# Eight plain first feed-forward tiles before twelve Strassen-Winograd pairs, the last gate's modulation inside the second product, and one more slot for weights

## Chip, cores and metric

The kernel runs on one core of a Trainium2 chip. The time is device microseconds of one execution. Three runs of the kernel before took 1071.28, 1064.88 and 1070.12 us; their median is 1070.12 us.

## What is computed

Two transformer blocks stand behind each other, for 512 tokens of width 1024, all in fp32. The first has 16 meta tokens ahead of the sequence, a pooling branch and an attention with forget gates; the second takes six modulation vectors (two shifts, two scales, two gates) from a conditioning vector `c`, has two kinds of attention, and a feed-forward part with a squared ReLU:

```python
def hybrid_layer(x, norm_g, w_in, b_forget, pool_w, pool_scale, w_up_pool, w_up_attn, w_out):
    h = rmsnorm(x, norm_g)
    proj = jnp.einsum('bld,dn->bln', h, w_in)
    ...
    merged = (jax.nn.sigmoid(g_pool) * jnp.einsum('blc,cd->bld', y_pool, w_up_pool)
              + jax.nn.sigmoid(g_attn) * jnp.einsum('blc,cd->bld', y_attn, w_up_attn))
    return x + jnp.einsum('bld,de->ble', merged, w_out)

def second_block(x, c, g_norm1, w_in, g_q, g_k, rel_bias, w_o, g_norm2, w1, w2, w_ada, b_ada):
    ...
        mod = c_act @ w_ada[l] + b_ada[l]
        sh1, sc1, gt1, sh2, sc2, gt2 = [m[:, None, :] for m in jnp.split(mod, 6, axis=-1)]
    ...
        x = x + gt1 * (mixed @ w_o[l])
        h = rmsnorm_2(x, g_norm2[l]) * (1.0 + sc2) + sh2
        x = x + gt2 * (jnp.square(jax.nn.relu(h @ w1[l])) @ w2[l])
```

`w_ada` is 1024 x 6144, `w1` 1024 x 4096, `w2` 4096 x 1024. The diff is about the sixth modulation vector, `gt2` (number 5 in the kernel), which is needed only at the very end, and about the products with `w1` and `w2`.

## The kernel before

**Products.** Every fp32 operand is split into a high and a low part (`split`, L130 to L132: ScalarE casts, L131, and VectorE or GpSimd subtracts, L128), and a product is three matmuls, high by high, high by low, low by high (`mm3`, L149 to L152). The order of TensorE's instructions is the order in which the code is written or woven (`manual_schedule`, `weave`); on the other engines a scheduler puts each instruction in its place, and every engine then works through its own list in order.

**Weights.** A weight tile of 512 KB comes by a DMA that SP issues into one of four slots with the tag `wr` (`weights`, L134; `w1_raw`, L1241). The cast writes one of three slots `wh`, the subtraction one of three slots `wl`. SP's list is in order too: an issue that waits for a slot holds all issues behind it.

**Modulation.** `ada(v, j)` (L203 to L217) brings one eighth of modulation vector `v`: a 512 KB load into a `wr` slot (issued at L207) and two VectorE ops, which add two rows of the weight tile, each multiplied by an entry of `c`, to the accumulator `ada` (L215 for the first, L217 for the others). After four steps one half of the vector lies there as 128 partial sums for each of 512 columns. `ada_end` (L219) sums over the partitions by TensorE (L234, eight matmul instructions in the trace for a half) and adds the bias (L237); for a gate a transpose on TensorE follows (L227), a copy, and a write to DRAM (L230), from which `load_gt` (L763) brings it back, spread over all partitions. The list `todo` holds the steps, and `ada_step(n)` takes up to n of them at set places: in block 1 vectors 0, 1, 3 and 5, three steps behind each of the eight output tiles `ups(m)` at its end; in block 2 vectors 4 and 2. `ada_all()` does what is left.

**First feed-forward product.** Its 32 tiles of 128 columns are made in two ways. A plain tile is 48 matmuls of 256 columns (`first_half`, twice). EARLY = 5 of them are done in two halves each, so that the first halves can start before the second half of the tokens is ready; one more plain tile follows. The other 26 tiles come as 13 pairs in Strassen and Winograd's form: seven products of 12 matmuls (`prod`, L1204 to L1206), 84 in all where two plain tiles have 96. For them VectorE makes four sums of the two weight tiles (`sums`, L1263 to L1266), each of which is split. A pair is `firsts` (two products), `middles` (three) and `lasts` (two), and `lasts` of a pair stands between `firsts` and `middles` of the next. `plus` (L1274 copy by ScalarE, L1275 sum by VectorE) joins two banks of PSUM into the hidden tile, and the next products that use these banks wait for it.

**Second product.** For each of 32 hidden tiles `w2_operands` loads and splits a row block of `w2` and the hidden tile, and 24 matmuls of 512 columns follow. The last two hidden tiles are done output by output, with the gate and the residual behind each.

## Time and profile before

| | us |
|---|---|
| three runs | 1064.88 to 1071.28, median 1070.12 |
| the profiled execution's own time | 1068.56 |
| its span in the trace | 1066.9 |
| TensorE busy in it | 1018.2 |
| VectorE, ScalarE, GpSimd busy | 610.4, 565.2, 297.3 |

The mean granted clock of TensorE in it is 0.992 of full speed; full speed (1.00) is 2.4 GHz, and the other level is half of it. A row of a timeline gives the start, the duration, the engine (PE is TensorE, DVE VectorE, ACT ScalarE, POOL GpSimd, SPq the list of SP), the source line, the operation with its output and inputs, and in brackets how long the engine was idle before it and what it waited for. Matmuls overlap, so the time that one costs is the distance between starts.

### The profile page before, as it was taken

The numbers are of one execution on the slowest core, as the hardware profiler recorded it, in microseconds if no ns is written. First come the engines' busy times: TensorE is split into PE (matmuls) and PEld (weight loads), VectorE is DVE, ScalarE is ACT, GpSimd is POOL, SyncE is SP. The second block draws the span as 40 slices with busy tenths as digits, with TensorE's granted clock in tenths as the row PEclk, the third lists the DMA queues.
The fourth block names the chain that finished last, engine by engine and source line by source line (L and its number), as shares of the span: only waits on it lengthen the run. The fifth ranks groups of instructions, "written<-read, shape, count | busy, mean of one in ns | idle before, by whom it ended". The sixth has DMA issues, their size and how long they took to land.

```text
span 1066.9 us, 15553 instructions
## 1 busy us (share of the span) xinstructions
PE 1018.2 (95%) x5923; PEld 862.1 (81%) x5923; DVE 610.4 (57%) x1183; ACT 565.2 (53%) x1089; POOL 297.3 (28%) x156
## 2 busy tenths in 40 slices
PE   7999999999998999899899988899899999999998
PEld 5987987778876788887678866689799998888886
DVE  5375866864365548566777577666667652111115
ACT  6365654554535646465677678446576773222221
POOL 4221124422322353112212114232222322333320
PEclk9999999999999999999999999999899999999999
DMA  8242532453564656416512134541233334233312
GB/s 239 84 119 63 150 115 80 138 162 96 157 178 131 212 181 203 141 40 179 156 53 77 50 98 134 161 119 47 81 100 111 111 88 139 79 99 99 99 60 79
DMA packets 133980, 125.54 MB, mean 118 GB/s; under 512 B 6053, under 2 KB 110337, under 8 KB 133906
## 3 DMA queue, kind: packets, MB, share of 16 engines
q1 hardware_dynamic: 133906, 124.56, 39.4%
q8 instruction: 46, 0.75, 0.3%
q14 instruction: 28, 0.23, 0.1%
HBM read 119.82 MB, written 4.73 MB: 117 GB/s over the span
## 4 chain that ended last, share of the span: by engine, by line
PE 66%; DVE 12%; DMA 8%; ACT 5%; issue 5%; POOL 3%; SPq 0%; DVEq 0%; ACTq 0%; POOLq 0%
PE ps L150 15%; PE ps L152 15%; PE ps L151 14%; DMA wr<-in_w_in_dram 5%; PE ps L1204 4%; PE ps L1205 4%; PE ps L1206 4%; POOL wl L128 3%; ACT wh L131 2%; PE ps L963 2%; DVE ada L217 1%; PE ps L519 1%; PE ps L438 1%; PE ps L916 1%; DMA wr<-in_w_up_attn_dram 1%
## 5 line engine op out<-in xcount | busy, mean ns | idle before, releaser
L128 POOL TENSOR_TENSOR wl<-wr,wh 128x1024 fp32r<-128x1024 f32 x98 | 244.6, 2499 | 640.1 <-ACT wh L131 609.4
L131 ACT CAST wh<-wr 128x1024 fp32r<-128x1024 f32 x129 | 135.0, 1048 | 222.5 <-issue 88.9
L150 PE MATMUL ps<-hh,wh 128*128 128x512 f32 (+1 forms) x352 | 130.3, 370 | 2.2 <-ACT wh L131 1.6
L152 PE MATMUL ps<-hh,wl 128*128 128x512 f32 (+1 forms) x352 | 125.5, 356 | 2.2 <-POOL wl L128 1.7
L151 PE MATMUL ps<-hl,wh 128*128 128x512 f32 (+1 forms) x352 | 125.4, 356 | 0.0
L150 PE MATMUL ps<-wh,T 128*128 128x512 f32 x256 | 100.9, 394 | 0.0
L152 PE MATMUL ps<-wh,T 128*128 128x512 f32 x256 | 100.8, 394 | 0.0
L151 PE MATMUL ps<-wl,T 128*128 128x512 f32 x256 | 100.5, 393 | 0.0
L150 PEld LDWEIGHTS ps<-hh,wh 128*128 128x128 f32 x352 | 66.6, 189 | 22.6 <-issue 10.8
L217 DVE SCALAR_TENSOR_TENSOR ada<-wr,vc,ada 128x512 f32<-128x512 f32 x84 | 76.2, 908 | 4.0 <-DMA wr<-in_w_ada_dram 2.9
L152 PEld LDWEIGHTS ps<-hh,wl 128*128 128x128 f32 x352 | 66.6, 189 | 12.8 <-POOL wl L128 2.1
L151 PEld LDWEIGHTS ps<-hl,wh 128*128 128x128 f32 x352 | 66.6, 189 | 7.7
L128 DVE TENSOR_TENSOR wl<-T,wh 128x512 fp32r<-128x512 f32 x52 | 37.3, 735 | 43.4 <-ACT wh L131 43.4
L128 DVE TENSOR_TENSOR wl<-wr,wh 128x1024 fp32r<-128x1024 f32 x31 | 39.9, 1287 | 35.9 <-ACT wh L131 35.9
L1205 PE MATMUL ps<-PT,wh 128*128 128x256 f32 x208 | 59.0, 284 | 0.0
L1204 PE MATMUL ps<-QK,wh 128*128 128x256 f32 x208 | 58.9, 283 | 0.0
L1206 PE MATMUL ps<-QK,wl 128*128 128x256 f32 x208 | 58.7, 282 | 0.0
L152 PEld LDWEIGHTS ps<-wh,T 128*128 128x128 f32 x256 | 48.1, 188 | 11.3
L151 PEld LDWEIGHTS ps<-wl,T 128*128 128x128 f32 x256 | 48.2, 188 | 11.1
L150 PEld LDWEIGHTS ps<-wh,T 128*128 128x128 f32 x256 | 48.1, 188 | 10.8
L150 PE MATMUL ps<-h2h,wh 128*128 128x512 f32 (+1 forms) x144 | 54.9, 382 | 0.0
L152 PE MATMUL ps<-h2h,wl 128*128 128x512 f32 (+1 forms) x144 | 53.6, 372 | 0.0
(407 smaller groups left out, 2669.0 us busy)
## 6 DMA issues: line engine op xcount, KB each, us to landing
wr<-in_w_in_dram SPq DMA_DIRECT2D x64, 512.0 KB, 4.9
wr<-in_w_dram SPq DMA_DIRECT2D x64, 512.0 KB, 3.6
wr<-in_w_ada_dram SPq DMA_DIRECT2D x48, 512.0 KB, 4.0
wr<-in_w_out_dram SPq DMA_DIRECT2D x12, 512.0 KB
wr<-in_w_o_dram SPq DMA_DIRECT2D x12, 512.0 KB, 3.6
xr<-in_x_dram SPq DMA_DIRECT2D x8, 512.0 KB, 5.0
wr<-in_w_up_pool_dram SPq DMA_DIRECT2D x8, 256.0 KB
wr<-in_w_up_attn_dram SPq DMA_DIRECT2D x8, 256.0 KB
```

The source lines that it names most:

```text
L128: (eng or pool).tensor_tensor(dst, raw, f(hi), op=OP.subtract)
L131: act.copy(dst_hi, raw)
L150: pe.matmul(ps, lh, rh, start=start, stop=False)
L151: pe.matmul(ps, lh, rl, start=False, stop=False)
L152: pe.matmul(ps, ll, rh, start=False, stop=stop)
L217: dve.scalar_tensor_tensor(acc, raw[:, q, :], cs, acc, op0=OP.mult, op1=OP.add)
L438: pe.matmul(ps, A[e][:, sa], B[e][:, sb], start=True, stop=False)
L519: pe.matmul(po[64 * e:64 * e + 64, c0:], lhs, rhs, start=j < 0, stop=j == 3)
L963: pe.matmul(ps[:, d0:], ntri if j2 == j else nones, part[:, SOFF[j2]:SOFF[j2] + 512 - d0], start=False, stop=part is sl and j2 == j, skip_ ...
L1204: pe.matmul(ps, wh, bh, start=first and k == 0, stop=False, **go)
L1205: pe.matmul(ps, wh, bl, start=False, stop=False, **go)
L1206: pe.matmul(ps, wl, bh, start=False, stop=k == 3, **go)
```

## The change

More slots: five `wr` instead of four, four `wh` and `wl` instead of three, six `T` instead of five; the room comes from a smaller scratch for DMA descriptors (`dynamic_dma_scratch_size`). PLAIN = 8 tiles of the first product are plain, three of them behind the two-half ones, and 12 pairs follow; the second halves of the five early tiles come in the order 2, 3, 4, 0, 1. Vector 5 leaves the list of block 1, where `ada_step(2)` stands instead of `ada_step(3)`; its eight steps are called in the loop of the second product, for hidden tiles 2 to 9. Its sums over partitions are no longer made by TensorE: `gate_sum` transposes blocks of 32 x 32 on VectorE, reduces, brings the four groups of 32 partitions together, reduces again, adds the bias (`gate_b`, a load of 32 x 32 single elements) and writes 512 single elements to DRAM. `load_gt` follows at hidden tile 10.

```diff
--- before.py
+++ after.py
@@ -132,7 +132,7 @@
         lo_of(dst_lo, raw, dst_hi, eng)
 
     def weights(aps, shape, hi=None, lo=None, eng=None):
-        raw = wts.tile([128] + shape, F32, name="wr", tag="wr", bufs=4)
+        raw = wts.tile([128] + shape, F32, name="wr", tag="wr", bufs=5)
         if len(aps) == 1:
             sp.dma_start(raw, aps[0])
         else:
@@ -140,8 +140,8 @@
             for i, x in enumerate(aps):
                 sp.dma_start(raw[:, i * n:(i + 1) * n, :], x)
         if hi is None:
-            hi = wts.tile([128] + shape, F32R, name="wh", tag="wh", bufs=3)
-            lo = wts.tile([128] + shape, F32R, name="wl", tag="wl", bufs=3)
+            hi = wts.tile([128] + shape, F32R, name="wh", tag="wh", bufs=4)
+            lo = wts.tile([128] + shape, F32R, name="wl", tag="wl", bufs=4)
         lo_turn[0] += 1
         split(hi, lo, raw, eng or (dve if lo_turn[0] % dve_turn[0] == 0 else pool))
         return hi, lo
@@ -202,7 +202,7 @@
 
     def ada(v, j):
         half, k = j // 4, 2 * (j % 4)
-        raw = wts.tile([128, 2, 512], F32, name="wr", tag="wr", bufs=4)
+        raw = wts.tile([128, 2, 512], F32, name="wr", tag="wr", bufs=5)
         x = a["w_ada_2"]
         sp.dma_start(raw, bass.AP(tensor=x.tensor, offset=x.offset + 128 * k * 6 * D + v * D + 512 * half,
                                   ap=[[6 * D, 128], [128 * 6 * D, 2], [1, 512]]))
@@ -269,7 +269,7 @@
     dram = ctx.enter_context(tc.tile_pool(name="dram", bufs=1, space=bass.MemoryType.DRAM))
     mx_d = [dram.tile([128, 512], F32, name=f"mx{q}_d") for q in range(4)]
     gate_d = {v: dram.tile([8, 128], F32, name=f"gate{v}_d") for v in (2, 5)}
-    BUFS = {"QK": 2, "PT": 3, "Y": 4, "V": 1, "T": 5, "Z": 2, "PTm": 2, "strip": 1, "Cm": 1, "Vm": 1}
+    BUFS = {"QK": 2, "PT": 3, "Y": 4, "V": 1, "T": 6, "Z": 2, "PTm": 2, "strip": 1, "Cm": 1, "Vm": 1}
 
     def wt(shape, tag, dt=F32):
         return work.tile(shape, dt, name=tag, tag=tag, bufs=BUFS[tag])
@@ -605,7 +605,7 @@
             if p < 3:
                 yield from qk1(p + 1)
                 ada_step(2)
-        raw = wts.tile([128, 4, 128], F32, name="wr", tag="wr", bufs=4)
+        raw = wts.tile([128, 4, 128], F32, name="wr", tag="wr", bufs=5)
         sp.dma_start(raw, bass.AP(tensor=a["pool_w"].tensor, offset=a["pool_w"].offset,
                                   ap=[[128, 128], [128 * 128, 4], [1, 128]]))
         pw = resid.tile([128, 2, 4, 128], F32R, name="pw", tag="xr", bufs=4)
@@ -621,9 +621,9 @@
             ada_step()
         for m in range(8):
             yield from ups(m)
-            ada_step(3)
-
-    todo += [(v, k) for v in (0, 1, 3, 5) for k in range(8)]
+            ada_step(2)
+
+    todo += [(v, k) for v in (0, 1, 3) for k in range(8)]
     UT = wt([128, NP], "T")
     pool.memset(UT, 1.0)
     pool.affine_select(UT, UT, pattern=[[1, NP]], base=0, channel_multiplier=-1, compare_op=OP.is_ge, fill=0.0)
@@ -1221,7 +1221,8 @@
 
     dve_turn[0] = TURN2
     w1x = a["w1_2"]
-    EARLY = 5
+    EARLY, PLAIN = 5, 8
+    SECOND = (2, 3, 4, 0, 1)
 
     def hid_out(ft, ps):
         act.activation(hid[ft], ps, AF.Relu)
@@ -1239,13 +1240,13 @@
         clk[0] += 2840
 
     def w1_raw(ft):
-        raw = wts.tile([128, D], F32, name="wr", tag="wr", bufs=4)
+        raw = wts.tile([128, D], F32, name="wr", tag="wr", bufs=5)
         sp.dma_start(raw.rearrange("p (k n) -> p k n", k=KT), wcols(w1x, FF, 128 * ft, 128))
         return raw
 
     def w_pair(n, tag_hi="wh", tag_lo="wl"):
         if n == 1024:
-            return wts.tile([128, n], F32R, name="wh", tag="wh", bufs=3), wts.tile([128, n], F32R, name="wl", tag="wl", bufs=3)
+            return wts.tile([128, n], F32R, name="wh", tag="wh", bufs=4), wts.tile([128, n], F32R, name="wl", tag="wl", bufs=4)
         return wt([128, n], "Z", F32R), wt([128, n], "PTm", F32R)
 
     H0, H1 = slice(0, 512), slice(512, 1024)
@@ -1313,15 +1314,16 @@
         first_half(halves[ft], first[ft], 0)
     wino_right(us)
     first_half(halves[EARLY - 1], first[EARLY - 1], 0)
-    for ft in range(EARLY):
+    for ft in SECOND:
         first_half(halves[ft], first[ft], 1)
         hid_out(ft, halves[ft])
     for g in range(2):
         wino_sums(g)
-    w, ps = weights([wcols(w1x, FF, 128 * EARLY, 128)], [KT, 128]), bank()
-    for q in range(2):
-        first_half(ps, w, q)
-    hid_out(EARLY, ps)
+    for ft in range(EARLY, PLAIN):
+        w, ps = weights([wcols(w1x, FF, 128 * ft, 128)], [KT, 128]), bank()
+        for q in range(2):
+            first_half(ps, w, q)
+        hid_out(ft, ps)
     held = []
 
     def w2_operands():
@@ -1331,7 +1333,7 @@
         split(hs[0], hs[1], hid[ft], dve)
         held.append((hs, ws))
 
-    for i in range((EARLY + 1) // 2, 16):
+    for i in range(PLAIN // 2, 16):
         ra, rb = w1_raw(2 * i), w1_raw(2 * i + 1)
         firsts(i, first_row(ra))
         ws = sums(ra, rb)
@@ -1342,9 +1344,22 @@
     lasts()
     if tap: tap("hid", hid[30])
 
-    ada_all()
-    load_gt(5, hid[31])
-    gt = gtp[5]
+    gate_b = consts.tile([32, 32], F32, name="gate_b")
+    sp.dma_start(gate_b, bass.AP(tensor=a["b_ada_2"].tensor, offset=a["b_ada_2"].offset + 5 * D, ap=[[1, 32], [32, 32]]))
+
+    def gate_sum(half):
+
+        acc = ada_acc[0]
+        tr, red, quads = tmp([128, 512]), sm([128, 16], "gs", 1), sm([32, 4, 16], "gq", 1)
+        dve.transpose(tr, acc)
+        dve.tensor_reduce(red, tr.rearrange("p (b c) -> p b c", c=32), axis=AX.X, op=OP.add)
+        for q in range(4):
+            dve.tensor_copy(quads[:, q, :], red[32 * q:32 * q + 32, :])
+        dve.tensor_reduce(red[:32], quads.rearrange("p q b -> p b q"), axis=AX.X, op=OP.add)
+        dve.tensor_tensor(red[:32], red[:32], gate_b[:, 16 * half:16 * half + 16], op=OP.add)
+        g = gate_d[5]
+        sp.dma_start(bass.AP(tensor=g.tensor, offset=g.offset + 512 * half, ap=[[1, 32], [32, 16]]), red[:32])
+
     po = [[bank(), bank()] for _ in range(2)] + [[bank(), bank()] for _ in range(2)]
     LAST = 2
 
@@ -1355,6 +1370,14 @@
     for ft in range(32):
         if ft:
             w2_operands()
+        if 2 <= ft < 10:
+            ada(5, ft - 2)
+            if ft % 4 == 1:
+                ada_due.pop()
+                gate_sum(ft // 4 - 1)
+        if ft == 10:
+            load_gt(5, hid[31])
+            gt = gtp[5]
         hs, ws = held[ft]
         if ft < 32 - LAST:
             for t in range(4):
@@ -1387,7 +1410,7 @@
     arrays = {n: np.ascontiguousarray(inputs[n]) for n in _INS}
     rel = np.clip(np.arange(128)[:, None] + 384 - np.arange(512)[None, :], -128, 128) + 128
     arrays["band"] = np.ascontiguousarray(np.asarray(inputs["rel_bias_2"])[0][:, rel])
-    nc = bacc.Bacc("TRN2", target_bir_lowering=False, num_devices=1)
+    nc = bacc.Bacc("TRN2", target_bir_lowering=False, num_devices=1, dynamic_dma_scratch_size=1024)
     aps = {n: nc.dram_tensor(f"in_{n}_dram", x.shape, mybir.dt.from_np(x.dtype), kind="ExternalInput").ap()
            for n, x in arrays.items()}
     out = nc.dram_tensor("out_0_dram", (1, S, D), F32, kind="ExternalOutput").ap()
```

SP's list in the last steps of block 1. Before, the last tiles of `w_in`, the up projections and a modulation load (L207) stand there:

```order
L137 DMA wr_3188<-in_w_in_dram 128x8x128
L137 DMA wr_3224<-in_w_in_dram 128x8x128
L141 DMA wr_3260<-in_w_up_pool_dram 128x4x128
L141 DMA wr_3260<-in_w_up_attn_dram 128x4x128
L207 DMA wr_3298<-in_w_ada_2_dram 128x2x512
L137 DMA wr_3303<-in_w_in_dram 128x8x128
L137 DMA wr_3339<-in_w_in_dram 128x8x128
L141 DMA wr_3375<-in_w_up_pool_dram 128x4x128
L141 DMA wr_3375<-in_w_up_attn_dram 128x4x128
L137 DMA wr_3447<-in_w_out_dram 128x1024
```

After the change, at the same place (from the `w_in` loads of `ups(6)` to the first `w_out` load):

```order
L141 DMA wr_3224<-in_w_up_pool_dram 128x4x128
L141 DMA wr_3224<-in_w_up_attn_dram 128x4x128
L137 DMA wr_3263<-in_w_in_dram 128x8x128
L137 DMA wr_3299<-in_w_in_dram 128x8x128
L141 DMA wr_3335<-in_w_up_pool_dram 128x4x128
L141 DMA wr_3335<-in_w_up_attn_dram 128x4x128
L137 DMA wr_3396<-in_w_out_dram 128x1024
L137 DMA wr_3414<-in_w_out_dram 128x1024
L137 DMA wr_3432<-in_w_out_dram 128x1024
```

No modulation load stands between the weight loads any more.

VectorE's list at the end of the pairs. `ps` tiles are banks of PSUM, `hid` the hidden tiles, `T` the sums and splits. Before, with the sums of `plus` at L1275 and those of `lasts` at L1303:

```order
L128 TENSOR_TENSOR wl_8838<-T_8844,wh_8837 128x512
L128 TENSOR_TENSOR wl_8838<-T_8843,wh_8837 128x512
L128 TENSOR_TENSOR T_8937<-PT_6870,T_8936 128x512
L1275 TENSOR_TENSOR hid_6877<-ps_8775,hid_6877 128x256
L128 TENSOR_TENSOR wl_8840<-T_8845,wh_8839 128x512
L1275 TENSOR_TENSOR hid_6877<-ps_8810,hid_6877 128x256
L128 TENSOR_TENSOR wl_8840<-T_8846,wh_8839 128x512
L128 TENSOR_TENSOR T_9014<-PT_6870,T_9013 128x512
L1303 TENSOR_TENSOR hid_6877<-ps_8775,hid_6877 128x256
L128 TENSOR_TENSOR wl_9010<-wr_9007,wh_9009 128x1024
L1275 TENSOR_TENSOR hid_6877<-ps_8903,hid_6877 128x256
L1303 TENSOR_TENSOR hid_6877<-ps_8903,hid_6877 128x256
```

After the change the same sums have the lines L1276 and L1304:

```order
L215 TENSOR_SCALAR ada_8984<-wr_8982,vc_89 128x512
L217 SCALAR_TENSOR_TENSOR ada_8984<-wr_8982,vc_89,ada_8984 128x512
L128 TENSOR_TENSOR T_8945<-PT_6819,T_8944 128x512
L128 TENSOR_TENSOR wl_8775<-T_8780,wh_8774 128x512
L1276 TENSOR_TENSOR hid_6826<-ps_8710,hid_6826 128x256
L128 TENSOR_TENSOR wl_8775<-T_8781,wh_8774 128x512
L128 TENSOR_TENSOR T_8979<-PT_6819,T_8978 128x512
L217 SCALAR_TENSOR_TENSOR ada_8984<-wr_9021,vc_89,ada_8984 128x512 x2
L1276 TENSOR_TENSOR hid_6826<-ps_8745,hid_6826 128x256
L1304 TENSOR_TENSOR hid_6826<-ps_8710,hid_6826 128x256
L217 SCALAR_TENSOR_TENSOR ada_8984<-wr_9059,vc_89,ada_8984 128x512 x2
L1276 TENSOR_TENSOR hid_6826<-ps_8838,hid_6826 128x256
```

The first modulation ops of the second product (L215, L217) now stand between the splits and ahead of the sums of the last two pairs.

VectorE's list near 50 to 65 us, where the L427 and L434 ops finish keys and queries of block 1's attention and L653 the sums of the log gates. Before:

```order
L427 SCALAR_TENSOR_TENSOR QK_610<-ps_617,QK_610 64x512
L217 SCALAR_TENSOR_TENSOR ada_809<-wr_1023,vc_89,ada_809 128x512
L427 SCALAR_TENSOR_TENSOR QK_610<-ps_617,QK_610 64x512
L434 SCALAR_TENSOR_TENSOR lz10_590<-ps_652,QK_610 64x264
L434 SCALAR_TENSOR_TENSOR lz11_591<-ps_652,QK_610 64x264
L217 SCALAR_TENSOR_TENSOR ada_809<-wr_1109,vc_89,ada_809 128x512 x2
L434 SCALAR_TENSOR_TENSOR lz10_590<-ps_683,QK_610 64x264
L653 TENSOR_TENSOR Cm_112<-ps_715,Cm_112 8x16
L434 SCALAR_TENSOR_TENSOR lz11_591<-ps_683,QK_610 64x264
L653 TENSOR_TENSOR Cm_112<-ps_714,Cm_112 8x512
```

After the change, from the third modulation tile on:

```order
L217 SCALAR_TENSOR_TENSOR ada_809<-wr_1023,vc_89,ada_809 128x512 x2
L217 SCALAR_TENSOR_TENSOR ada_809<-wr_1109,vc_89,ada_809 128x512 x2
L427 SCALAR_TENSOR_TENSOR QK_610<-ps_617,QK_610 64x512 x2
L434 SCALAR_TENSOR_TENSOR lz10_590<-ps_652,QK_610 64x264
L434 SCALAR_TENSOR_TENSOR lz11_591<-ps_652,QK_610 64x264
L434 SCALAR_TENSOR_TENSOR lz10_590<-ps_683,QK_610 64x264
L653 TENSOR_TENSOR Cm_112<-ps_715,Cm_112 8x16
L434 SCALAR_TENSOR_TENSOR lz11_591<-ps_683,QK_610 64x264
L653 TENSOR_TENSOR Cm_112<-ps_714,Cm_112 8x512
```

The two ops on the fourth modulation tile, `wr_1109`, moved from between the L434 ops to ahead of both L427.

## Rows read from the trace of the kernel before

**Rows 1.** The page, part 1: engine, busy us, share of the span, instructions
```profile
PE 1018.2 (95%) x5923; PEld 862.1 (81%) x5923; DVE 610.4 (57%) x1183; ACT 565.2 (53%) x1089; POOL 297.3 (28%) x156
```

**Rows 2.** Timelines, first pair: start, us, engine, instruction [idle before <-releaser]
```profile
741.16 0.39 PE L152 MATMUL ps<-QK,wl 128*128 128x256 f32 x1 [0.45 <-POOL wl L128]
...
749.50 0.28 PE L1206 MATMUL ps<-QK,wl 128*128 128x256 f32 x1
754.96 0.58 PE L1204 MATMUL ps<-tsum,wh 128*128 128x256 f32 x1 [5.18 <-DVE Y L1275]
...
759.39 0.31 PE L1206 MATMUL ps<-QK,wl 128*128 128x256 f32 x1
...
751.04 0.37 ACT L1274 COPY Y<-ps 128x256 f32<-128x256 f32 x1
```

**Rows 3.** Windows: us, busy of each engine (x instructions), PEclk, DMA share, GB/s
```profile
340.00:360.00 20.00, 16.88 (x66) 13.06 (x66) 8.90 (x18) 11.03 (x16) 7.10 (x3) 0.91 0.91 293
740.00:760.00 20.00, 14.37 (x101) 13.96 (x101) 8.97 (x11) 6.32 (x13) 6.26 (x3) 0.83 0.49 131
780.00:800.00 20.00, 20.00 (x170) 20.00 (x170) 13.70 (x24) 14.13 (x27) 5.49 (x3) 1.00 0.39 108
900.00:920.00 20.00, 20.00 (x88) 16.25 (x87) 4.00 (x5) 6.28 (x8) 5.54 (x3) 1.00 0.34 106
```

**Rows 4.** Timelines of SP's queue and ScalarE, block 1's last steps
```profile
337.61 0.37 SPq L207 DMA_DIRECT2D wr<-in_w_ada_dram  x1
...
343.35 1.04 ACT L131 CAST wh<-wr 128x1024 fp32r<-128x1024 f32 x1 [5.90 <-DMA wr<-in_w_in_dram]
```

**Rows 5.** Timeline of TensorE, block 1's last steps
```profile
344.44 0.50 PE L150 MATMUL ps<-hh,wh 128*128 128x512 f32 x1 [1.41 <-ACT wh L131]
...
346.88 0.80 PE L152 MATMUL ps<-hh,wl 128*128 128x512 f32 x1 [1.70 <-POOL wl L128]
...
349.94 0.39 PE L150 MATMUL ps<-hh,wh 128*128 128x512 f32 x1
```

**Rows 6.** Timeline of TensorE, column sums and gate transpose
```profile
364.54 0.95 PE L234 MATMUL ps<-ones_f,ada 128*128 128x1 f32 x8
366.18 0.27 PE L227 MATMUL ps<-ident,mod 128*8 128x128 f32 x1 [0.69 <-DVE mod L237]
```

**Rows 7.** Timeline of VectorE, 48 to 60 us
```profile
49.09 0.75 DVE L217 SCALAR_TENSOR_TENSOR ada<-wr,vc,ada 128x512 f32<-128x512 f32 x1
...
55.52 0.69 DVE L427 SCALAR_TENSOR_TENSOR QK<-ps,QK 64x512 fp32r<-64x512 f32 x1
...
59.49 3.56 DVE L217 SCALAR_TENSOR_TENSOR ada<-wr,vc,ada 128x512 f32<-128x512 f32 x2
```

**Rows 8.** Waits of TensorE: us in total, times, longest us
```profile
PE ps L879 <- DVE PTm L128: 5.0, 5, 2.2
...
PE ps L481 <- DVE Cm L653: 1.2, 1, 1.2
```

**Rows 9.** The page, part 3: packets, MB, share of 16 engines
```profile
q1 hardware_dynamic: 133906, 124.56, 39.4%
```

**Rows 10.** The page, part 5: busy us, mean ns of one | idle before
```profile
L128 POOL TENSOR_TENSOR wl<-wr,wh 128x1024 fp32r<-128x1024 f32 x98 | 244.6, 2499 | 640.1 <-ACT wh L131 609.4
...
L217 DVE SCALAR_TENSOR_TENSOR ada<-wr,vc,ada 128x512 f32<-128x512 f32 x84 | 76.2, 908 | 4.0 <-DMA wr<-in_w_ada_dram 2.9
```

**Rows 11.** Timeline of TensorE, pair 14; the page's DMA issues (us to landing)
```profile
863.91 0.28 PE L1204 MATMUL ps<-lz,Z 128*128 128x256 f32 x1
...
wr<-in_w_ada_dram SPq DMA_DIRECT2D x48, 512.0 KB, 4.0
```

**Rows 12.** Timelines of SP's queue, VectorE and TensorE, start of block 2
```profile
406.62 9.50 SPq L207 DMA_DIRECT2D wr<-in_w_ada_dram  x4
...
413.11 1.31 DVE L215 TENSOR_SCALAR ada<-wr,vc 128x512 f32<-128x512 f32 x1 [2.82 <-DMA wr<-in_w_ada_dram]
...
415.87 0.39 PE L152 MATMUL ps<-Y,h2l 128*128 128x256 f32 x1 [1.97 <-DVE h2l L673]
```

## Prediction

> **What bounds the kernel now.** I read the engine totals first: TensorE is busy for 1018.2 of 1066.9 us and no other engine for over 611 [rows 1]. So time is won only by fewer matmuls, by less idle on TensorE, or by fewer stretches at the half clock. Next came the table of TensorE's waits and its timeline around the places that the diff touches. Third came the two queues that feed those waits: SP, which issues all loads, and VectorE, where one late instruction holds everything behind it. Durations are those of the profiled execution, 1068.56 us; its span is 1066.9, and the 1.7 outside I leave alone. It lies 1.6 under the median of 1070.12, inside the spread of 1064.88 to 1071.28. About 1% either way, some 10.7 us, is what a measurement of this kernel can tell from no change, so under 1059.4 counts as faster.
>
> **More plain tiles, one pair fewer.** At its first pair TensorE issues the last `firsts` matmul at 749.50 and the next one at 754.96, 5.18 of it put down to VectorE's sum at L1275 (L1276 after the change); and from there to 759.39 it starts 21 matmuls, 0.22 apart instead of 0.118 [rows 2]. The clock of that stretch was granted at 0.83 of full speed on the mean, against 1.00 in the steady pairs [rows 3], so part of it ran at 1.2 GHz instead of 2.4. Twenty distances in 4.43 us against 20 x 20.00/170 = 2.35 is 2.1 lost. Just before, the one plain tile waits 0.45 for its low part. The cause is cover: one plain tile is 48 matmuls x 0.118 = 5.7 us, and in it ScalarE and VectorE must make a whole pair's sums and cuts from loads that have just landed. Afterwards three plain tiles stand there, 17 us, so the operands are ready. But a first pair has no previous pair's `lasts` between its `firsts` and its `middles`; the copy at L1274 can't start before the last `firsts` product ends, and it came 1.54 after 749.50 [rows 2]. With the copy (0.37), VectorE's sum and the two hand-overs I keep 2.1 of wait, with no half clock. Gain: 5.18 + 0.45 + 2.1 - 2.1 = 5.6. Were the sums still late it would be 0; were TensorE to wait for nothing, 7.7. The price is Strassen-Winograd's saving: two plain tiles are 96 matmuls, a pair 84, so 12 x 0.118 = 1.4 more, and this is certain. The new order of the second halves (2, 3, 4, 0, 1) issues the same instructions; I give it nothing.
>
> **One modulation out of block 1.** In its last steps TensorE waits twice and then runs slow, and the SP queue says why: a modulation load is issued at 337.61, when a slot is free, and the two projection loads stand right behind it; ScalarE's cast waits 5.90 for one of them and starts at 343.35 [rows 4]. TensorE then waits 1.41 and 1.70, and goes at half clock from 346.88 to 349.94, 3.06 for seven distances that take 7 x 20.00/88 = 1.6 at full speed [rows 5, 3]; the window from 340 to 360 shows 0.91. After the change this stage has 24 modulation loads instead of 32, two per step instead of three, and five slots instead of four; in the last three steps SP has only weight loads. I take the three terms as gone: 1.4 + 1.7 + 1.45 = 4.55; bounds 0 (the loads are late for another reason) and 4.55. Waits of half a microsecond elsewhere in the stage I don't count. The column sums leave with certainty: eight L234 matmuls and the gate's transpose run from 364.54 to 366.18, which is 1.64, and the other half's eight cost up to 0.95, of which I take 0.8 [rows 6]. That is 2.45. Each wait that goes also returns the part of the gap outside its bracket; at 754.96 this is 5.46 - 0.12 - 5.18 = 0.16, so 0.6 for the four (0.45, 1.41, 1.70 and the 1.2 below).
>
> **The early part.** VectorE's two L217 at 59.49 take 3.56 because a load is late [rows 7], and the sum L653 behind them hands 1.2 to TensorE [rows 8]. In the changed order these two stand further ahead, in front of both L427, and the sum waits for no load: 1.2 gained. Now L427 stands behind the load. Its slot is free after the op at 49.09, say 49.9; 4.0 later it has landed, its two ops end at 55.4, and the first L427 started at 55.52 [rows 7]: no delay. At 6.47 to landing it would be 2.4 late, so the bounds are a gain of 1.2 and a loss of 1.2. The new load of the gate's bias is 1024 elements of four bytes. The queue's average packet cost 39.4% x 16 x 1066.9 / 133,906 = 50 ns of one engine [rows 9], so 1024 over 16 engines are 3.2 us, if each is an average one. Nothing waits for it until the second product, and the loads behind it run into slots anyway: I take 0, bounds 0 and 3.2. The Trainium skill (Perfetto Trace Analysis, DMA Optimizations) says that transfers under 2 KB carry significant overhead each. No run so far shows four-byte ones; by that rule the upper bound would be taken, and the sum would end 3.2 higher.
>
> **The last gate in the second product.** There VectorE is busy 4.00 of 20 us beside a TensorE that never waits [rows 3]. Eight loads, 16 ops of some 0.9 [rows 10] and two sums add about 18 us over 44: hidden. But the scheduler puts the first of them earlier. In the changed order of VectorE the loads' ops stand ahead of sums of pairs 14 and 15 (the block of the change's section). I take the clock of before: the `firsts` of pair 14 end at 863.91 [rows 11]. The first load gets its slot when POOL has cut pair 15's first row, a cast of 1.04 and a cut of 2.5 later [rows 4, 10], at about 867.7; 4.0 to landing [rows 11] gives 871.7, and its two ops end at 873.0, which nobody notices. The second load takes the same slot, so 873.1, 877.1, two ops, 878.6, then the sum: 878.95. TensorE wants it after 108 matmuls, 863.91 + 108 x 0.1187 = 876.7. That is a new wait of 2.2. A third load ends some 0.3 beyond what is there anyway. I take +2.5. Below nothing it can't be; with the landing of 6.47 that the row below shows it is 2.0 + 5.3 + 2.2 and some 2 of half clock, 11.5.
>
> The precedent is in the trace: at 413.11 VectorE's L215 ended a wait of 2.82 for a load issued at 406.62, and TensorE waited 1.97 for the L673 behind it [rows 12]. That place itself stays: L215 stands a little earlier there now. I put 0, with 2 either way.
>
> The Trainium skill (DMA: Bandwidth & Descriptors, Anatomy of one DMA) prices a transfer at about 2.0 us plus its bytes at 436 GB/s, an estimate of 3.2 for 512 KB. The trace's 4.0 disagrees, and 6.47 still more. By the page's price the new wait would be 0.6 and the sum 1.9 lower.
>
> **The sum.** -5.6 + 1.4 - 4.55 - 2.45 - 0.6 - 1.2 + 2.5 = -10.5; 1068.56 - 10.5 = 1058.1. More slots for weights carry no term of their own: they are in the stalls that go.
>
> **Rivals.** First, the slower side: VectorE's queue turns the gate's landing times into TensorE waits. Two chained loads and a third make each microsecond of landing beyond 4.0 cost about 2.8 (11.5 - 2.5 - 2 of half clock, over 2.5). For it speaks rows 12, where the first of four loads issued together took 6.47; against it, that at the end of the pairs loads come singly and the queues are 0.3 to 0.4 busy [rows 3]. At 6.47 the kernel ends at 1058.1 + 9 = 1067.1. From about 6.9 the gain is gone; at 8 us the wait is 2.5 + 2.8 x 4.0 + 4 of half clock = 17.7, and the kernel ends at 1073.3, slower than before.
>
> Second, the stalls of block 1 have another cause. The cast that waited 5.90 would then wait for its own chain of slots, and only the column sums leave: 4.55 and 0.3 less, and 1063.0. For it: the projection loads were issued directly behind the modulation load, which costs SP 0.37 [rows 4], and the DMA engines are 0.91 busy from 340 to 360 [rows 3], so that a load may be slow whatever stands ahead of it. Against: the slot itself came late, and a modulation load keeps one until VectorE has used it.
>
> Third, the fifth raw slot and the fourth pair of slots also shorten waits that I left alone, 5.0 at L879 [rows 8] and 1.97 at L673 [rows 12]. Most of these end on VectorE's own work, which speaks against. Were 5 of those 7 to go, 1053.1.
>
> **How the numbers follow.** The forecast with its own bounds of 1054.5 to 1062: 0.50. The second rival: 0.20. The third: 0.13. The first, from 1063 up: 0.17, of which 0.07 ends above 1070. The range reaches from 1050 to 1067.5 and leaves out the first rival's worse half and some of the third. Faster by over 1% needs under 1059.4: seven tenths of the forecast's case and the third rival, 0.48. Slower by over 1% needs over 1080.8, a landing of 9 us and more or a queue in the second product that I don't see: 0.05. The rest, 0.47, is within 1%.
>
> **What would show it.** Right, if TensorE's gap at the first pair is near 2 us and the clock there stays at 1.00; if the last block-1 tile starts without a wait; if L234 counts 80 instead of 96; if two waits for VectorE's L1276 stand at the end of the pairs, about 2.2 and under 1, with VectorE idle before L217 until a modulation load lands; and if the second product shows a full TensorE with VectorE at about 8 of 20. The prediction is wrong if the waits at the end of the pairs add up to over 5, if the first pair still waits over 4, or if the projections of block 1's last steps still come late.

## The result, and the profile after

The changed kernel takes 1057.76 us (median of 4 runs, 1057.25 to 1058.66), the kernel before beside it 1069.42 (4 runs). The ratio is 0.9898, with a 95% interval of 0.9866 to 0.9931. Forecast were 1058.1 and a range of 1050 to 1067.5. The time came out as forecast, but several terms of the sum did not; they cancelled, so that an agreement to 0.3 us is in good part luck. The profiled execution took 1057.35, with a span of 1055.2.

The engine totals after, against [rows 1]: TensorE has 5.4 us less of busy time and, with a span 11.7 shorter, 6.3 less of idle.

```profile
PE 1012.8 (96%) x5918; PEld 857.8 (81%) x5918; DVE 628.3 (60%) x1184; ACT 561.8 (53%) x1082; POOL 301.0 (29%) x157
```

Where the 11.65 came from is read off the start of the same matmul in both timelines of TensorE:

| matmul | before | after | shift | step | forecast for the step |
|---|---|---|---|---|---|
| first L481, block 1 | 65.69 | 64.87 | -0.82 | -0.82 | -1.4 |
| last L519, block 1's values | 219.06 | 220.47 | +1.41 | +2.23 | 0 |
| first of `w_out`, block 1 | 366.20 | 358.76 | -7.44 | -8.85 | -7.3 |
| last L664, block 2's entry | 435.13 | 425.07 | -10.06 | -2.62 | 0 |
| last `Y`, `mxs`, block 2 | 696.92 | 686.05 | -10.87 | -0.81 | 0 |
| first L150 of the second product | 884.58 | 873.64 | -10.94 | -0.07 | -1.85 |
| last matmul | 1062.05 | 1050.40 | -11.65 | -0.71 | 0 |

TensorE's waits after (total, times, longest):

```profile
PE ps L1204 <- DVE hid L1276: 5.4, 1, 5.4
...
PE ps L879 <- DVE PTm L128: 4.6, 4, 1.5
...
PE ps L519 <- ACT PT L504: 3.1, 1, 3.1
...
PE ps L1204 <- DVE V L1276: 1.7, 1, 1.7
...
PE ps L152 <- DVE h2l L673: 0.6, 2, 0.4
PE ps L481 <- DVE Cm L653: 0.5, 1, 0.5
```

The first and the third of these have taken the place of what went: one at the end of the pairs, one in block 1. The windows of the same stages (columns as in [rows 3]; each stage starts some 8 to 11 earlier now):

```profile
340.00:360.00 20.00, 20.00 (x88) 16.18 (x87) 10.81 (x16) 12.26 (x17) 4.26 (x2) 1.00 0.52 185
730.00:750.00 20.00, 18.60 (x162) 18.40 (x160) 11.51 (x17) 10.32 (x19) 3.59 (x2) 1.00 0.38 104
...
860.00:880.00 20.00, 15.25 (x88) 13.90 (x89) 9.77 (x14) 7.72 (x12) 6.26 (x3) 0.91 0.40 134
900.00:920.00 20.00, 20.00 (x89) 16.32 (x88) 13.14 (x16) 6.30 (x8) 7.77 (x3) 1.00 0.88 223
```

Block 1's last steps are full and at full clock (16.88 busy and 0.91 before), the first pair has kept the full clock (0.83 before), and the loss sits at 860 to 880. In the second product TensorE is full; VectorE is busy 13.14 of 20 from 900 to 920, since three of the four tiles of the gate's second half, and its sums, fall there. L234 counts 80 instead of 96, as forecast.

The chain of waits through the end of the pairs (start, us, what):

```profile
849.72 4.04 DMA wr<-in_w_ada_dram
...
855.08 3.64 DMA wr<-in_w_ada_dram
...
858.74 2.42 DVE ada L217
861.19 2.71 DVE ada L217
863.89 0.35 DVE hid L1276
...
864.28 0.58 PE ps L1204
```

The loads landed as forecast, in 4.04 and 3.64. The two ops behind the second one did not run as forecast: 2.42 and 2.71, where the same op takes 0.75 by itself. The timelines of the engines there, and at the first pair, show what else ran:

```profile
858.25 5.10 POOL L128 TENSOR_TENSOR wl<-wr,wh 128x1024 fp32r<-128x1024 f32 x2 [8.56 <-ACT wh L131]
...
854.30 0.75 DVE L217 SCALAR_TENSOR_TENSOR ada<-wr,vc,ada 128x512 f32<-128x512 f32 x1
...
858.74 5.15 DVE L217 SCALAR_TENSOR_TENSOR ada<-wr,vc,ada 128x512 f32<-128x512 f32 x2 [0.76 <-DMA wr<-in_w_ada_dram]
...
864.28 0.58 PE L1204 MATMUL ps<-tsum,wh 128*128 128x256 f32 x1 [5.41 <-DVE hid L1276]
...
867.61 0.28 PE L1204 MATMUL ps<-QK,wh 128*128 128x256 f32 x1
...
750.30 0.39 PE L1204 MATMUL ps<-tsum,wh 128*128 128x256 f32 x1 [1.70 <-DVE V L1276]
```

GpSimd made two cuts from 858.25 to 863.35, and VectorE's two ops lie beside them. TensorE waited 5.41 and then issued 15 matmuls in 3.33 us, 0.22 apart. At the 0.118 of the steady pairs they are 1.77, so 1.6 more went at 1.2 GHz, and the place costs 7. Why the op is so long was the first question for the runs; the second was which part of the change earned what.

### The profile page after: what moved, and what is told of

It reads as the page before. It is cut to its first block, busy times and chain, and to the rows that moved or that the text cites. A ratio compares the mean times of both kernels' runs of the same rounds, so it can differ in the third digit from the quotient of the medians.

```text
span 1055.2 us, 15524 instructions
## 1 busy us (share of the span) xinstructions
PE 1012.8 (96%) x5918; PEld 857.8 (81%) x5918; DVE 628.3 (60%) x1184; ACT 561.8 (53%) x1082; POOL 301.0 (29%) x157
## 4 chain that ended last, share of the span: by engine, by line
PE 76%; DVE 9%; issue 5%; ACT 3%; DMA 3%; POOL 3%; SPq 0%; DVEq 0%; POOLq 0%; ACTq 0%
PE ps L150 19%; PE ps L152 18%; PE ps L151 18%; PE ps L1204 4%; PE ps L1206 3%; PE ps L1205 3%; DVE ada L217 2%; PE ps L963 2%; DMA wr<-in_w_ada_dram 2%; POOL wl L128 1%; DMA wr<-in_w_in_dram 1%; PE ps L519 1%; PE ps L438 1%; PE ps L439 1%; DVE QK L427 1%
## 5 line engine op out<-in xcount | busy, mean ns | idle before, releaser
L128 POOL TENSOR_TENSOR wl<-wr,wh 128x1024 fp32r<-128x1024 f32 x99 | 248.1, 2511 | 577.7 <-ACT wh L131 567.1
L131 ACT CAST wh<-wr 128x1024 fp32r<-128x1024 f32 x130 | 136.3, 1050 | 106.5 <-PE ps L151 55.7
L150 PE MATMUL ps<-hh,wh 128*128 128x512 f32 (+1 forms) x352 | 129.7, 368 | 0.0
L150 PE MATMUL ps<-wh,T 128*128 128x512 f32 x256 | 101.0, 394 | 0.0
L217 DVE SCALAR_TENSOR_TENSOR ada<-wr,vc,ada 128x512 f32<-128x512 f32 x84 | 81.7, 972 | 11.4 <-DMA wr<-in_w_ada_dram 10.4
L150 PEld LDWEIGHTS ps<-hh,wh 128*128 128x128 f32 x352 | 66.3, 188 | 20.4 <-issue 11.5
L128 DVE TENSOR_TENSOR wl<-wr,wh 128x1024 fp32r<-128x1024 f32 x31 | 41.4, 1336 | 29.1 <-ACT wh L131 29.1
L150 PEld LDWEIGHTS ps<-wh,T 128*128 128x128 f32 x256 | 48.1, 188 | 10.6
L150 PE MATMUL ps<-h2h,wh 128*128 128x512 f32 (+1 forms) x144 | 54.9, 381 | 0.0
L1206 PE MATMUL ps<-QK,wl 128*128 128x256 f32 x192 | 53.7, 280 | 0.0
L1204 PE MATMUL ps<-QK,wh 128*128 128x256 f32 x192 | 53.7, 279 | 0.0
L1205 PE MATMUL ps<-PT,wh 128*128 128x256 f32 x192 | 53.4, 278 | 0.0
L151 PE MATMUL ps<-h2l,wh 128*128 128x512 f32 (+1 forms) x144 | 53.1, 369 | 0.0
```

Of the source, the lines that this page charges most:

```text
L128: (eng or pool).tensor_tensor(dst, raw, f(hi), op=OP.subtract)
L131: act.copy(dst_hi, raw)
L150: pe.matmul(ps, lh, rh, start=start, stop=False)
L151: pe.matmul(ps, lh, rl, start=False, stop=False)
L217: dve.scalar_tensor_tensor(acc, raw[:, q, :], cs, acc, op0=OP.mult, op1=OP.add)
L1204: pe.matmul(ps, wh, bh, start=first and k == 0, stop=False, **go)
```

## The experiments

Each ratio is against the kernel before on the same chip. Experiments 1 to 4 shared one chip, 5 to 8 one, 9 to 11 one.

### One part at a time

**1. Plain tiles alone**, in the kernel before.

```diff
-    EARLY = 5
+    EARLY, PLAIN = 5, 8
+    SECOND = (2, 3, 4, 0, 1)
```

with the two loops and the range of the pairs as in the change.

> The kernel before with eight plain tiles, the new order of the second halves and 12 pairs, nothing else. My theory: the stall at the first pair shrinks from 5.2 to about 2 us and its half clock goes, because three plain tiles cover the sums whatever the number of slots; 1.4 us of matmuls are added; the stalls near 345 us, 416 us and 65 us stay as before. Time 4 to 5 us under before, about 1065. Rival: with four raw slots the loads for the first pair are held up by those of the plain tiles, so TensorE still waits over 4 us there and the time is that of before or 1 us more.

1067.01, ratio 0.9970 [0.9951, 0.9989]: 2.7 under the kernel before, where 4 to 5 were expected. The first pair waits as after the change, and block 1's two stalls stay:

```profile
PE ps L1204 <- DVE V L1276: 1.8, 1, 1.8
PE ps L150 <- ACT wh L131: 1.8, 2, 1.6
PE ps L152 <- POOL wl L128: 1.7, 1, 1.7
```

**2. The slots alone**, in the kernel before.

```diff
-        raw = wts.tile([128] + shape, F32, name="wr", tag="wr", bufs=4)
+        raw = wts.tile([128] + shape, F32, name="wr", tag="wr", bufs=5)
-            hi = wts.tile([128] + shape, F32R, name="wh", tag="wh", bufs=3)
+            hi = wts.tile([128] + shape, F32R, name="wh", tag="wh", bufs=4)
-    BUFS = {"QK": 2, "PT": 3, "Y": 4, "V": 1, "T": 5, "Z": 2, "PTm": 2, "strip": 1, "Cm": 1, "Vm": 1}
+    BUFS = {"QK": 2, "PT": 3, "Y": 4, "V": 1, "T": 6, "Z": 2, "PTm": 2, "strip": 1, "Cm": 1, "Vm": 1}
```

and the same for `wl`, the other `wr` tiles and the smaller scratch, as in the change.

> The kernel before with five raw slots, four slots for high and low parts and six for T, nothing else. My theory: the slots alone take part of the stalls of block 1's last steps (3.1 us and 1.5 of half clock before) and of block 2's entry (2.0), since loads can be issued earlier, but the modulation loads still stand ahead of the projection loads: 2 to 4 us gained, about 1066; the first pair still waits about 5 us. Rival 1: all of the gain in block 1 and block 2 is the slots' (8 to 10 us, about 1060). Rival 2: without taking out the modulation the slots do nothing (1068 to 1071).

1054.07, ratio 0.9856 [0.9827, 0.9886]: a lower median than the whole change, with intervals that overlap, and 12 us under what was expected here. With the gate still in block 1 the window from 340 to 360 is full, and with one plain tile the first pair waits 2.0 and keeps its clock, where 5 us were expected. Its own new wait is the one at L519:

```profile
PE ps L519 <- ACT PT L504: 3.2, 1, 3.2
...
PE ps L1204 <- DVE Y L1275: 2.0, 1, 2.0
```

```profile
340.00:360.00 20.00, 20.00 (x92) 16.30 (x90) 12.13 (x16) 13.76 (x20) 3.52 (x2) 1.00 0.65 234
730.00:750.00 20.00, 18.01 (x152) 17.80 (x151) 15.08 (x22) 9.58 (x19) 5.28 (x2) 1.00 0.39 107
```

So the slots by themselves reach at least what the whole change does, and the prediction gave them no term of their own.

**3. The gate's move alone**, in the kernel before.

```diff
-            ada_step(3)
+            ada_step(2)
-    todo += [(v, k) for v in (0, 1, 3, 5) for k in range(8)]
+    todo += [(v, k) for v in (0, 1, 3) for k in range(8)]
```

with `gate_sum` and the calls in the second product as in the change.

> The kernel before with the last gate's modulation moved into the second product and summed by VectorE, with the old slots and the old 13 pairs. My theory: the column sums and the gate's transpose go (2.5 us) and with them most of the stalls of block 1's last steps (about 5); the first pair waits 5 us as before; at the end of the pairs the modulation ops stand later in VectorE's order than in the changed kernel, so TensorE waits there under 2 us instead of 5.4. About 1062. Rival: with four slots the gate's loads and the weights of the second product get into each other's way and TensorE waits in the second product; time 1066 or more.

1061.01, ratio 0.9924 [0.9893, 0.9954]. The stalls of block 1 are gone here too; the first pair waits 6.2 and runs slow, and at the end of the pairs TensorE waits 1.1:

```profile
340.00:360.00 20.00, 20.00 (x88) 16.19 (x87) 9.53 (x15) 11.50 (x15) 3.04 (x2) 1.00 0.54 185
730.00:750.00 20.00, 13.17 (x101) 12.77 (x100) 8.96 (x11) 6.34 (x13) 6.23 (x3) 0.83 0.51 132
```

**4. The change without the gate's move.**

```diff
-            ada_step(2)
+            ada_step(3)
-    todo += [(v, k) for v in (0, 1, 3) for k in range(8)]
+    todo += [(v, k) for v in (0, 1, 3, 5) for k in range(8)]
```

with `ada_all` and `load_gt` back where they were.

> The changed kernel with the last gate's modulation back in block 1 and its sums on TensorE; plain tiles and slots as changed. My theory: no wait of 5.4 us and no half clock at the end of the pairs (7 us better there), but the column sums (2.5) and part of the stalls of block 1 (2 to 4) come back: about 1057 to 1060, so the gate's move is worth next to nothing in all. Rival: the stalls of block 1 come back whole and the time is 1062 or more.

1056.20 (1054.20 to 1057.52), ratio 0.9870 [0.9846, 0.9894]. No wait stands at the end of the pairs. The intervals of this and of the whole change overlap, so that the move costs 1.5 inside the change is not certain; no gain of it shows there.

**5. The change without the plain tiles**: `SECOND` and `PLAIN` back to five early tiles, one plain one and 13 pairs.

> Slots and the gate's move as changed, but one plain tile and 13 pairs as before. My theory, after the first four runs: the slots already supply the cover at the first pair, so here too TensorE waits only about 2 us there, and the changed kernel's two more plain tiles cost 1.4 us of matmuls and some 0.7 beside: about 2 us faster than the changed kernel, 1055.5. Rival: with the gate's loads out of block 1 the order differs and the first pair waits 5 us again: 1059 or more.

1055.92 (1054.70 to 1059.81), ratio 0.9874 [0.9848, 0.9899]: not told apart from the change. The first pair waits 4.0 now, and the end of the pairs 3.4. The 1055.5 of the expectation is met by luck: it rested on a first pair that waits 2.

Alone, the three parts are worth 2.7, 15.7 and 8.7, which is 27; together they are worth 11.7. They remove the same waits, and the gate brings a new one.

### What the wait at the end of the pairs is

**6. The gate later**, in the changed kernel: hidden tiles 8 to 15 in place of 2 to 9.

```diff
-        if 2 <= ft < 10:
-            ada(5, ft - 2)
-            if ft % 4 == 1:
+        if 8 <= ft < 16:
+            ada(5, ft - 8)
+            if ft % 4 == 3:
 ...
-                gate_sum(ft // 4 - 1)
-        if ft == 10:
+                gate_sum(ft // 4 - 2)
+        if ft == 16:
 ...
```

> The changed kernel with the gate's eight steps at hidden tiles 8 to 15 instead of 2 to 9 and load_gt at 16; in VectorE's order no modulation op stands before the last sum of the pairs then. My theory: the wait of 5.4 us and the 1.5 us at half clock at the end of the pairs go and nothing comes in their place: 7 us faster than the changed kernel, about 1051. Rival: the wait comes back in the second product, where the modulation ops then stand ahead of cuts and hidden tiles that TensorE needs: 1055 or more.

1050.84 (1050.22 to 1051.67), ratio 0.9820 [0.9805, 0.9836], 6.9 under the change. Against experiment 4, the change without the move, it is 5.4 lower, and the two intervals lie apart: once its wait is gone, the move does earn something. The wait is gone, the clock stays, and the second product hides all of the gate:

```profile
860.00:880.00 20.00, 19.54 (x110) 16.87 (x110) 3.18 (x7) 9.80 (x14) 7.80 (x4) 1.00 0.44 132
880.00:960.00 80.00, 80.00 (x349) 65.32 (x348) 40.44 (x51) 22.11 (x28) 27.51 (x11) 1.00 0.56 143
```

**7. GpSimd taken away from that place**, in the changed kernel: VectorE makes the two cuts.

```diff
-        ws = weights([rows(a["w2_2"], 128 * ft, 128, D, 0, D)], [D], eng=dve if ft == 31 else None)
+        ws = weights([rows(a["w2_2"], 128 * ft, 128, D, 0, D)], [D], eng=dve if ft in (0, 1, 31) else None)
```

> The changed kernel with the low parts of the first two row blocks of the second product cut by VectorE instead of GpSimd, so that GpSimd is idle while VectorE works on the second modulation tile near 859 us. Theory A: there VectorE's two L217 took 5.15 us instead of 1.5 because GpSimd's cuts held the reading port that both need; without them they take 0.75 each, one cut of 1.3 is added on VectorE, and TensorE's wait falls from 5.4 to about 3, with no half clock: about 1054. Theory B: the two ops are slow because of the transfers into the slots; then they still take about 5 us and TensorE waits over 6: 1059.

1055.87, ratio 0.9866 [0.9849, 0.9884]. GpSimd does nothing until 867.33 here, the load lands at the same time as after the change, and the two ops behind it take 1.54 in place of 5.15:

```profile
858.59 1.54 DVE L217 SCALAR_TENSOR_TENSOR ada<-wr,vc,ada 128x512 f32<-128x512 f32 x2 [0.86 <-DMA wr<-in_w_ada_dram]
860.04 1.22 DVE L128 TENSOR_TENSOR wl<-wr,wh 128x1024 fp32r<-128x1024 f32 x1
...
861.65 0.39 PE L1204 MATMUL ps<-tsum,wh 128*128 128x256 f32 x1 [3.07 <-DVE hid L1276]
```

The wait is 3.07 and not less, because one of the cuts now stands ahead of the sum on VectorE itself, 1.22. That settles it for this place: the long ops were waiting for GpSimd, and not for the load. The time is 1.9 above theory A's, which had no half clock; the window behind this wait still has 3.2 us of it.

The Trainium skill (SBUF — State Buffer, SBUF: two separate sides) says that a VectorE op with two inputs in SBUF and a GpSimd op share a pair of ports that is held for a whole instruction, so that the other engine stands still. L217 reads the slot and the sum, both in SBUF; the cut L128 reads the slot and the high part. The trace agrees: 2.42 and 2.71 beside a cut of 2.55, 0.75 and 0.77 without one.

**8. Late gate and slots, without the plain tiles**: experiment 6 with five early tiles, one plain one and 13 pairs.

> The kernel before with the slots of the change and the gate in the second product from hidden tile 8 on, one plain tile and 13 pairs. My theory: the best of the parts: the slots' gain (15 us to 1054), the column sums and block 2's entry (3.5 us), no wait at the end of the pairs, and no extra matmuls: about 1050 to 1051. Rival: the gains of the slots and of the gate are the same ones, so that together they are worth no more than the slots: 1053 to 1055.

1053.01 (1048.71 to 1054.36), ratio 0.9833 [0.9802, 0.9864]. The first pair waits 4.05 here, and the timelines show the same pair of ports the other way round:

```profile
723.88 10.79 POOL L128 TENSOR_TENSOR wl<-wr,wh 128x1024 fp32r<-128x1024 f32 x1 [21.62 <-ACT wh L131]
734.90 2.40 POOL L128 TENSOR_TENSOR wl<-wr,wh 128x1024 fp32r<-128x1024 f32 x1 [0.24 <-ACT wh L131]
...
739.14 0.69 DVE L1263 TENSOR_TENSOR T<-wr 128x512 f32<-128x512 f32 x1 [6.71 <-DMA wr<-in_w_dram]
...
741.54 0.38 PE L1204 MATMUL ps<-tsum,wh 128*128 128x256 f32 x1 [4.05 <-DVE Y L1275]
```

A cut of 2.40 takes 10.79: VectorE runs one two-input op after the other from before its start until 732.4, and the cut ends 2.2 later. That the one holds up the other is read from these times; no run takes VectorE's ops away. Until the cut ends its slot is held, SP issues the next load at 734.69, and VectorE stands in front of that load at L1263 with L1275, which TensorE wants, behind it. With the gate out of block 1 the first pair waits 4.0 and 4.1 (experiments 5 and 8), with it there 2.0 (experiment 2), so that there the plain tiles may be of use: 2.2 between this run and experiment 6, with ranges that overlap. The time lies in the range of the rival.

### The new wait in block 1, and which slot it is

At L519 the timelines show where the 3.1 comes from (the first row is of the kernel before, the others of the changed one):

```profile
204.03 4.96 POOL L555 TENSOR_TENSOR T<-T 128x527 f32<-128x527 f32 x4
...
203.75 2.58 POOL L128 TENSOR_TENSOR wl<-wr,wh 128x1024 fp32r<-128x1024 f32 x1
206.30 2.43 POOL L555 TENSOR_TENSOR T<-T 128x521 f32<-128x521 f32 x2
...
208.76 0.69 DVE L558 SCALAR_TENSOR_TENSOR T<-T 128x512 f32<-128x512 f32 x1 [4.21 <-POOL T L555]
...
209.49 0.62 ACT L131 CAST xp<-T 128x512 fp32r<-128x512 f32 x1 [4.65 <-DVE T L558]
210.01 1.07 ACT L504 COPY PT<-ps 128x512 f32<-128x512 f32 x2
...
211.16 1.20 PE L519 MATMUL ps<-PTm,Vm 16*64 16x512 f32 x4 [3.15 <-ACT PT L504]
```

A weight cut stands in the middle of GpSimd's four window sums (L555). The last sum comes 2.6 later, ScalarE's cast waits for it, and the copy that TensorE wants stands behind the cast. In the kernel before the four sums stand together.

**9. The last group's window sums on VectorE**, on top of experiment 6.

```diff
-            pool.tensor_tensor(s[:, 2 * w - 1:], prev[:, 2 * w - 1:], prev[:, w - 1:NP - w], op=OP.add)
+            (dve if g == 3 else pool).tensor_tensor(s[:, 2 * w - 1:], prev[:, 2 * w - 1:], prev[:, w - 1:NP - w], op=OP.add)
```

> The kernel with the later gate (all parts of the change, gate steps at hidden tiles 8 to 15) and one more edit: the four window sums of the last pooling group (L555) are made by VectorE instead of GpSimd. In every run with the new slots TensorE waits 3.15 us near 211 us for ScalarE's copy at L504, which stands behind a cast of that group's result; GpSimd has slipped a weight's cut of 2.6 between its four sums. My theory: with the sums on VectorE the group's result comes 3 us sooner, the wait of 3.15 and the half clock behind it (1 to 2 us) go: about 1047. Rival: the sums delay VectorE's softmax steps of the attention there, and TensorE waits as long for those: 1050 to 1052.

1049.35 (1048.88 to 1050.74), ratio 0.9801 [0.9784, 0.9818]. The wait at L519 is gone, and one of 2.17 stands at L501, for VectorE, which has the sums now. The median is 1.5 under experiment 6, half of the 3.1 that were to be had and less than the 1047 expected; the intervals overlap.

**10. The fifth raw slot alone**, in the kernel before: `wr` 5, with the smaller scratch; `wh`, `wl` and `T` as before.

> The kernel before with five raw slots wr instead of four; wh, wl and T as before. My theory: loads are what comes late in block 1's last steps and at block 2's entry, so the raw slot brings most of the slots' 15 us: about 1057; the wait of 3.15 near 211 us needs the fourth wh and wl slot and is not there. Rival: the cuts' slots decide, and this gives under 4 us.

1051.95 (1051.55 to 1054.26), ratio 0.9831 [0.9811, 0.9850]. This one slot does all that the three kinds of slots did, 5 us more than expected, and the wait of 3.2 at L519 is not there; the intervals of this run and of experiment 2 overlap. The interval lies wholly under that of the change.

**11. The fourth slots for the parts alone**, in the kernel before: `wh` and `wl` 4, with the smaller scratch; the rest as before.

> The kernel before with four slots wh and wl instead of three; wr and T as before. My theory: a small gain of 2 to 5 us (1064 to 1067), since the loads still wait for raw slots, which now are freed sooner by earlier casts and cuts; the first pair still waits 4 to 5 us. Rival: these slots bring most of the 15 us: 1058 or less.

1064.52, ratio 0.9944 [0.9922, 0.9966]. Block 1's stalls stay, with 16.15 busy of 20 and the clock at 0.91:

```profile
340.00:360.00 20.00, 16.15 (x62) 12.40 (x62) 15.41 (x27) 12.64 (x18) 7.64 (x3) 0.91 0.70 211
```

The time is the expected one, but the first pair waits 2.0 where 4 to 5 were expected. GpSimd's four window sums stand together here, from 204.27 on, and TensorE waits 0.95 and then 1.95 for VectorE near them. So neither the raw slot nor the parts' slots make the wait of 3.2 by themselves; the sixth `T` was not tried alone.

**12. What the runs point to**: the changed kernel with the late gate of experiment 6, and of the slots the raw one only (`wh`, `wl` 3, `T` 5).

> Five raw slots, but three wh and wl and five T as in the kernel before; eight plain tiles; the gate in the second product from hidden tile 8 on. My theory: the fifth raw slot brings the gain of the slots without the wait of 3.15 us near 211 us, plain tiles give the cover at the first pair, and the late gate takes 2.5 us of column sums and has no wait at the end of the pairs: 1045 to 1047, the fastest of all. Rival: with the raw slot alone the gains of plain tiles and gate are the same ones again, and the time is that of the raw slot alone, 1051 to 1053.

1047.98 (1047.50 to 1048.41), ratio 0.9792 [0.9767, 0.9817]: the lowest time here, with an interval that overlaps those of experiments 6 and 9. Block 1's last steps are full (20.00 from 340 to 360); the first pair waits 1.8, and the end of the pairs is full:

```profile
730.00:750.00 20.00, 18.20 (x158) 18.00 (x157) 6.89 (x11) 9.64 (x18) 4.78 (x2) 1.00 0.37 102
860.00:880.00 20.00, 20.00 (x94) 16.42 (x93) 3.95 (x7) 7.74 (x10) 5.29 (x3) 1.00 0.34 109
```

GpSimd's four window sums stand together again there, and the wait at 206 is the 1.3 of the kernel before. In the second product TensorE waits 0.83 at 935.44 for a cut on VectorE that stands behind two modulation ops.

## Why the prediction was right, and where it was wrong

**Block 1's last steps: right.** The stalls and the column sums gave 8.85 where 7.3 was forecast. The cause, a raw slot that a modulation load holds, is borne out from two sides: one more slot removes the stalls with the loads still there (experiments 2 and 10), and the loads' absence removes them with four slots (experiment 3), while more slots for the parts don't (experiment 11). The second rival falls with this. What the prediction missed is that the two edits do the same thing: once the slot is there, the gate's move takes only the column sums out of these steps.

**The first pair: right in size, half wrong in cause.** The wait fell from 5.18 to 1.70, with no half clock; 2.1 was forecast. But "the cause is cover" is too much: with one plain tile the wait is 2.0 with all new slots, 1.8 with the fifth raw one (whose plain tile waits 1.6 ahead of it) and 2.0 with those for the parts (experiments 2, 10 and 11). Moving the gate makes it longer, to 6.2 with the old slots and 4.0 with the new ones (3 and 5), which the prediction did not see. In the kernel before, a load is late, and port and queue seem to add to it:

```profile
751.22 2.80 POOL L128 TENSOR_TENSOR wl<-wr,wh 128x1024 fp32r<-128x1024 f32 x1 [7.77 <-ACT wh L131]
...
745.49 0.69 DVE L1263 TENSOR_TENSOR T<-wr 128x512 f32<-128x512 f32 x1 [6.65 <-DMA wr<-in_w_dram]
...
751.86 2.71 DVE L1263 TENSOR_TENSOR T<-wr 128x512 f32<-128x512 f32 x1
754.50 0.41 DVE L1275 TENSOR_TENSOR Y<-ps,Y 128x256 f32<-128x256 f32 x1
```

The first L1263 waits 6.65 for its load; the second one, 2.71 for an op of 0.68, lies beside a cut and directly ahead of the L1275 that TensorE waits for. How much of the 5.18 each of them makes is not shown.

**The end of the pairs: place and order right, price wrong.** The term "that is a new wait of 2.2 ... I take +2.5" measured 7. The queue, the two landings and the ops behind the first one came as told, and the third load, put at 0.3, makes no wait. The step that failed is "877.1, two ops, 878.6": 1.5 for the second pair of ops, twice the 0.75 of [rows 7] and less than twice the mean of 908 ns in [rows 10], where 5.15 was measured. With 1.54 the sum would have ended at 860.7 and TensorE have waited 1.8. The other 3.6 of wait and the 1.6 of half clock behind it had no term. By its own test, over 5 in all at this place, the prediction is wrong here, whatever the total says. The price of 3.2 for a load, which the prediction takes from the Trainium skill (DMA: Bandwidth & Descriptors, Anatomy of one DMA), did not hold either: that section's fit is for transfers issued by GpSimd, and these, issued by SP, took 4.04 and 3.64. The first rival named this place as the slower side, but by the landing time, and the landing was 4.04 and 3.64.

**The same error, read in the trace of before.** [rows 7] shows two L217 of 3.56 at 59.49, and the prediction says that they are long "because a load is late". GpSimd's cut stands beside the second of them, and a third case stands in block 2:

```profile
60.00 2.49 POOL L128 TENSOR_TENSOR wl<-wr,wh 128x1024 fp32r<-128x1024 f32 x1 [24.06 <-ACT wh L131]
...
476.65 2.38 POOL L128 TENSOR_TENSOR wl<-wr,wh 128x1024 fp32r<-128x1024 f32 x1 [20.90 <-ACT wh L131]
...
476.62 2.97 DVE L217 SCALAR_TENSOR_TENSOR ada<-wr,vc,ada 128x512 f32<-128x512 f32 x1
...
481.06 0.36 PE L438 MATMUL ps<-QK 128*128 128x256 f32 x1 [2.52 <-DVE QK L427]
```

In these rows a late load stands in the bracket (2.82 at 413.11, 6.65 at 745.49), not in the op's duration. A price of some 2.9 for one op beside a cut was there to be read. That the cut holds these two up is read from the trace; only the end of the pairs was tested by a run. The gain at this place was 0.82 of 1.4; the wait at L481 is 0.5 now.

**What had no term.** The wait at L519 and slow matmuls behind it cost 2.2: "More slots for weights carry no term of their own" failed in this direction too, as experiments 2, 10 and 12 show (3.2, 1.3 and 1.3 at this place; the 1.3, at L501, is there in the kernel before too). The entry of block 2 gave 2.6, where "I put 0, with 2 either way" stood: the modulation op waits 1.93 where it waited 2.82 [rows 12], and TensorE 0.6 for L673 in place of 1.97. That is the slots' work: 0.6 and 0.2 with them (experiments 2 and 10), 2.1 with the gate's move alone (3). The third rival was right here, in part; of its 5.0 at L879 only 0.4 went. Block 2 gave 0.8 more, and the wait at 481.06 is gone.

**The twelve extra matmuls.** Between block 2's end and the second product the time is the same to 0.07. The first pair gave 6.1 (5.46 - 1.98 of gap, 2.1 of half clock, 0.5 of the gap at 741.16), the end of the pairs took 7.0; so the extra matmuls and all else there come to -1.0, not +1.4. The twelve themselves cost what was forecast: plain matmuls start as far apart as those of the pairs. What went the other way is this distance, at the same granted clock (after the change; [rows 3] has 170 for before):

```profile
780.00:800.00 20.00, 20.00 (x173) 20.00 (x173) 16.56 (x25) 14.18 (x27) 5.12 (x3) 1.00 0.40 106
```

From 0.1188 on the mean it went to 0.1171; over some 1,390 matmuls that is -2.4, and +1.4 - 2.4 is the -1.0. The gate's move brings it: this window holds 173 in all eight runs with the gate in the second product, and 170 to 172 in the six with it in block 1. Why, no run shows. The second product, where TensorE waits in neither kernel, gained its 0.7 in the same way: 767 distances of 0.2305 instead of 0.2314.

The sum, forecast against measured, is thus -1.4 and -0.8 early, 0 and +2.2 at L519, -7.3 and -8.85 in block 1's last steps, 0 and -3.4 in block 2, -1.85 and -0.1 in the pairs, 0 and -0.7 in the second product: -10.5 and -11.65.

## What to carry to other kernels

Before an op with two inputs in SBUF is put on VectorE, look at what GpSimd runs beside it: here 0.75 became 2.4 to 3.0, and a cut of 2.4 became 10.8. When several edits remove the same wait, time each alone; here one more raw slot was worth more than all edits together as they stood. Give work that is to be hidden a place that the scheduler can't draw ahead of a sum which another engine awaits: six hidden tiles later it made TensorE wait nowhere with the new slots (experiment 6), and 0.83 with the raw one alone (12).
